# First stage of a bidirectional mLSTM mixer: which projections accumulate while the modulated input is being made, and which engine makes the first two modulation tiles

## The chip, the cores and the metric

The kernel runs on one core of one Trainium2 chip. The metric is the device time of one execution in microseconds, taken as the median of several executions. The core's engines run their own instruction streams and meet through semaphores: TensorE (PE, with its weight loads as PEld), VectorE (DVE), ScalarE (ACT), GpSimd (POOL) and SyncE (SP), which issues the DMAs.

## The reference, cut to what matters

```python
mod = silu(c) @ w_mod + b_mod                  # 1024 -> 6*1024: sh1, sc1, ga1, sh2, sc2, ga2
mod_c = silu(c_ctx) @ w_mod + b_mod            # only csh1, csc1 are used
hx = rmsnorm(x, g_mix) * (1 + sc1) + sh1       # 1024 latent tokens x 1024
hc = rmsnorm(ctx, g_mix) * (1 + csc1) + csh1   # 256 context tokens
q, k, v, o, gates = split(h @ w_in)            # 4 heads: q, k of 128, v of 256; o of 1024; 16 gates
...                                            # mLSTM scans in both directions from the context state,
...                                            # readout, w_out, residual, ConvGLU with w_up and w_down
return rmsnorm(x, g_final)
```

Everything is float32. The change touches only what stands up to the gates' first scan (the rows on mod, hx, hc and the first part of `h @ w_in`).

## The kernel before, in words

A float32 product runs as three fast products (`mm3`): each factor is split into a high part (a cast by ACT) and a low part (a subtraction by DVE); `split` does that for a weight piece, `hx_make` for the modulated input. The hidden dimension of 1024 is cut into eight k tiles of 128. `hxh[k]` and `hxl[k]` hold k tile k for 256 context tokens followed by 1024 latent tokens.

The first stage makes these tiles. For each of eight token tiles, x is loaded, its sum of squares is taken on ACT (`normed`, L162), the scale is computed on POOL, x is scaled on ACT (L164), transposed on TensorE (`x_trans`, L175, eight 128x128 blocks into two PSUM tiles of the tag s0, which has two buffers), and copied by ACT into `xT` (L176). Beside it the two modulation vectors are made group by group (`GROUPS`: k tile 0, k tile 1, then pairs). `mod_load` fetches eight row blocks of w_mod for the group's columns into `mr` pieces (3 buffers); `mod_acc` has DVE add them, each times its element of silu(c) (L207 the first, L209 the others); `mod_done` has TensorE sum over the partitions with a vector of ones (L218) and DVE add the bias and gains (L221, L222). Only then can `hx_make` modulate k tile k on DVE (L229), cast on ACT (L230) and subtract on DVE (L231).

While the tiles arrive, `start_mm` accumulates v and o of head 0 (512 columns) for the first NT0 = 6 token tiles in six PSUM tiles `ac`, k tile by k tile; the weights are split per pair of k tiles (`vo_split`). After the last k tile come, from line 816 on (`cmods`, `gates_w` and the loop behind them): v and o of the last two token tiles (`pv`), q of head 0 (`pq`), the gates (`pg`, with a 32-column weight and 512 tokens moving), k of head 0 (`pk`), and between them the sums for the context's two modulation vectors (`mod_sum`, 16 pieces of 128x1024, DVE L772, closed by `mod_cols`, L780). Then the context is normed and transposed (`ctx_x`, L501), its gates are made, `gate_cols` turns the gates to token-major by transposes (`gp`, L473), and `gate_rows` computes the scan's coefficients (`grp` L523 to `cp` L562) while k and v of the context and q of head 1 fill TensorE. The first product behind that is head 1's k on the context.

Instructions stand in each engine's queue in an order that a scheduler derives from the written order and from buffers; an engine takes them strictly in turn. `raw_tile` has 3 buffers, `wtile` 8.

Of the kernel before, what the change touches and what calls it, by code (L numbers as in the profile page):

```python
# [16 lines left out]
P = 128  # L17
# [22 lines left out]
def backbone(ctx, tc, x, c, ctxt, c_ctx, w_mod, b_mod, g_mix, g_ffn, w_in, b_gate,  # L40
# [92 lines left out]
    vp = tc.alloc_tile_pool(name="vp", bufs=1, side="right")  # L133
# [22 lines left out]
    def x_load(t):
        xt[t] = sp.tile([P, D], F32, tag="x", bufs=3, name=f"xt{t}")
        nc.sync.dma_start(out=xt[t], in_=x[t * P:(t + 1) * P, :])

    def normed(a, junk, ms, name):  # L160
# [21 lines left out]
    def mod_load(g, i):  # L182

        ks = GROUPS[g]
        n = len(ks) * P
        nk = 512 // n
        m_ = sp.tile([P, nk, 2, n], F32, tag="mr", bufs=3, name=f"mr{g}_{i}")
# [4 lines left out]
        pieces[g, i] = m_  # L192

# [17 lines left out]
    def mod_done(g):  # L211

        ks = GROUPS[g]
        p_ = s0(f"mc{g}")
        for w in range(2):
            for i, k in enumerate(ks):
                j = w * len(ks) + i
                T.matmul(p_[:, 2 * j:2 * j + 2], accs[g][:, j * P:(j + 1) * P], ones[:, 0:2], start=True, stop=True)  # L218
        for i, k in enumerate(ks):
            j = len(ks) + i  # L220
            V.tensor_tensor(out=hmod[:, k, 0:1], in0=p_[:, 2 * i:2 * i + 1], in1=bmc[:, k:k + 1], op=ALU.add)  # L221
            V.scalar_tensor_tensor(out=smod[:, k, 0:1], in0=p_[:, 2 * j:2 * j + 1], scalar=b1[:, k:k + 1],  # L222
                                   in1=gmix[:, k:k + 1], op0=ALU.add, op1=ALU.mult)

    def hx_make(k, a, b):

        v_ = xT[:, k, a * P:b * P]
        h_, l_ = [q[k][:, CTX + a * P:CTX + b * P] for q in (hxh, hxl)]
        V.tensor_scalar(out=v_, in0=v_, scalar1=smod[:, k, 0:1], scalar2=hmod[:, k, 0:1], op0=ALU.mult, op1=ALU.add)  # L229
        S.copy(h_, v_)  # L230
        V.tensor_tensor(out=l_, in0=v_, in1=h_.bitcast(F32), op=ALU.subtract)  # L231

# [12 lines left out]

    NT0 = 6
    ac = [ps0.tile([P, 512], F32, tag="ac", bufs=NT0, name=f"ac{t}") for t in range(NT0)]
    w0 = []
# [78 lines left out]
    x_load(6)
    mod_acc(3, 2)
    mod_load(4, 0)
    w0 += vo_split(0, 2, raws[2])  # L330
    x_load(7)
    mod_acc(3, 3)
    mod_load(4, 1)
    mod_done(3)
    for k in (4, 5):
        hx_make(k, 0, NT0)
        start_mm(k, range(NT0))
        x_norm(k + 2)
# [50 lines left out]
    for t in range(NT0):  # L389
        vo_out(0, t + 2, ac[t])  # L390
# [33 lines left out]
    def proj_t(h, key, sls, wts=None):  # L424

        off, scale = (OFF_Q, 1.0) if key == "q" else (OFF_K, DK ** -0.5)
        dst = hd[h].get(key)
        if dst is None:
            dst = hp.tile([P, SEQ if key == "q" else TOK], F32, tag=f"{key}T", bufs=2, name=f"{key}T{h}")
            hd[h][key] = dst  # L430
        c0 = CTX if key == "q" else 0
        wh, wl = wts or wcols(off + h * DK, DK, f"w{key}{h}_")
        hd[h][key, "w"] = wh, wl
        for o, n in sls:
# [5 lines left out]
            S.mul(dst[:, o - c0:o - c0 + n], p_[:, :n], scale)  # L440
# [5 lines left out]


    gts = hp.tile([P, TOK], F32, tag="kT", bufs=2, name="gts")[:32, :]
    wg = hp.tile([P, KT, 32], F32R, tag="mb", bufs=4, name="wg")

    def gates_w():
        r_ = hp.tile([P, KT, 16], F32, tag="mb", bufs=4, name="wgr")
        nc.sync.dma_start(out=r_, in_=kp(w_in[:, OFF_G:OFF_G + 16]))
        S.copy(wg[:, :, 0:16], r_)
        V.tensor_tensor(out=wg[:, :, 16:32], in0=r_, in1=wg[:, :, 0:16].bitcast(F32), op=ALU.subtract)
        nc.sync.dma_start(out=bgate, in_=b_gate[0].partition_broadcast(P))

    def gates(sls):
        for o, n in sls:
            p_ = pj(f"pg{o}")  # L460
            for k in range(KT):
                T.matmul(p_[:32, :n], wg[:, k, :], hxh[k][:, o:o + n], start=k == 0, stop=False)
                T.matmul(p_[:32, :n], wg[:, k, :], hxl[k][:, o:o + n], start=False, stop=k == KT - 1)
                if k == 3:
                    yield
            S.copy(gts[:, o:o + n], p_[:32, :n])
            yield

    def gate_cols():

        gp = st("gp")
        for t in range(NCH):
# [878 lines left out]
```

## Time and profile before

| | |
|---|---|
| median of 3 executions | 1258.0 us (1257.34 to 1263.27) |
| the profiled execution's own time | 1259.66 us |
| its span, first to last instruction | 1257.9 us |
| TensorE busy | 1196.4 us, 95% |
| VectorE busy | 917.6 us, 73% |
| ScalarE busy | 521.5 us, 41% |

The profile is of one execution. Its page gives the engines' busy time and, in 40 slices of the span, the busy share and TensorE's granted clock. From the trace behind it come a table by stretches, the waits of each engine with what ended them, groups of instructions with their mean duration, and a timeline of single instructions. A matmul's duration reaches into the next one; its cost in a stream is the distance of two starts.

### The profile page before, as it was taken

How to read it: one execution, taken by the hardware profiler on the slowest of the kernel's cores; microseconds unless marked ns; L12 is line 12 of the kernel's file. 1: busy time of each engine (PE TensorE's matmuls, PEld its weight loads, DVE VectorE, ACT ScalarE, POOL GpSimd, SP SyncE). 2: the span in 40 equal slices, each digit the busy share in tenths (PEclk: the TensorE clock that was granted, in tenths of full speed). 3: DMA queues.
4: the chain of work that ended last, by engine and by line, in shares of the span. 5: the costliest groups of instructions: out<-in, count | busy, mean ns of one | idle time of the engine just before them, and what ended most of it. 6: DMA issues, size and time to landing. Idle time of an engine off the chain costs nothing. (4 is left out here: it accounts for less than half of the span.)

```text
span 1257.9 us, 15855 instructions
## 1 busy us (share of the span) xinstructions
PE 1196.4 (95%) x5657; PEld 986.9 (78%) x5657; DVE 917.6 (73%) x1575; ACT 521.5 (41%) x931; POOL 83.6 (7%) x212
## 2 busy tenths in 40 slices
PE   4998899999999998989899999999999999999996
PEld 3775788888888877878668888888888888888885
DVE  5774587488557437846898777777978877895787
ACT  6531646344335434426643333332333324444452
POOL 1100001001101100101500000000000000000001
PEclk9898899999999999999899999999999999999998
DMA  8735551066323107123123322325354469624523
GB/s 250 258 100 188 173 178 49 27 191 201 112 67 109 51 9 258 52 84 128 57 84 101 101 72 80 101 67 198 127 177 167 134 217 388 249 95 144 184 71 117
DMA packets 132067, 170.35 MB, mean 135 GB/s; under 512 B 8718, under 2 KB 93966, under 8 KB 131988
## 3 DMA queue, kind: packets, MB, share of 16 engines
q1 hardware_dynamic: 131988, 169.34, 40.9%
q8 instruction: 44, 0.72, 0.2%
q14 instruction: 35, 0.29, 0.1%
HBM read 134.67 MB, written 34.64 MB: 135 GB/s over the span
## 5 line engine op out<-in xcount | busy, mean ns | idle before, releaser
L1082 ACT ACTIVATE t<-gt,cols 128x1024 f32<-128x1024 f32 x22 | 27.4, 1245 | 63.8 <-DVE gt L980 63.8
L980 DVE TENSOR_TENSOR e<-e,p 128x512 f32<-128x512 f32 x66 | 44.8, 680 | 9.5 <-PE p L87 9.3
L980 DVE TENSOR_TENSOR gt<-e,p 128x512 f32<-128x512 f32 x66 | 44.8, 680 | 6.5 <-PE p L87 6.4
L125 POOL TENSOR_SCALAR fms<-fms 128x1 f32<-128x1 f32 x8 | 3.8, 474 | 612.4 <-PE pa L87 589.0
L1088 ACT ACTIVATE t<-t 128x1024 f32<-128x1024 f32 x22 | 23.4, 1063 | 48.4 <-DVE t L1085 48.4
L85 PE MATMUL pk<-hxh,wk_0h 128*128 128x512 f32 (+1 forms) x96 | 35.8, 375 | 6.0 <-ACT wk_0h L80 6.0
L728 DVE SCALAR_TENSOR_TENSOR ha<-ha,hms,so 128x256 f32<-128x256 f32 x32 | 15.5, 485 | 32.9 <-POOL hms L126 32.2
L1083 DVE SCALAR_TENSOR_TENSOR t<-gt,cols,t 128x960 f32<-128x960 f32 x22 | 26.7, 1214 | 13.2 <-ACT t L1082 13.2
L86 PE MATMUL pk<-hxh,wk_0l 128*128 128x512 f32 (+1 forms) x96 | 35.3, 368 | 0.0
L87 PE MATMUL pk<-hxl,wk_0h 128*128 128x512 f32 (+1 forms) x96 | 34.8, 363 | 0.0
L85 PE MATMUL p<-bt,av 128*128 128x512 f32 x88 | 34.2, 389 | 0.0
L86 PE MATMUL p<-bt,av 128*128 128x512 f32 x88 | 34.2, 389 | 0.0
L87 PE MATMUL p<-bt,av 128*128 128x512 f32 x88 | 34.2, 389 | 0.0
L379 DVE TENSOR_TENSOR vl<-pv,vh 128x256 fp32r<-128x256 f32 x34 | 14.2, 417 | 26.2 <-ACT vh L378 26.2
L378 ACT CAST vh<-pv 128x256 fp32r<-128x256 f32 x34 | 12.6, 370 | 47.1 <-PE pv L87 46.8
L85 PE MATMUL nm<-vh,wh 128*128 128x258 f32 x64 | 29.9, 468 | 0.0
L636 DVE SCALAR_TENSOR_TENSOR kl<-kt,cco,kh 128x128 fp32r<-128x128 f32 x44 | 15.1, 346 | 18.6 <-ACT kh L635 18.5
L694 ACT ACTIVATE wi<-mb,bco 128x128 f32<-128x128 f32 x64 | 23.6, 397 | 12.1 <-PE nm L711 11.9
L721 ACT ACTIVATE ha<-nm,dn 128x256 f32<-128x256 f32 x32 | 15.1, 473 | 32.0 <-DVE dn L719 31.9
L980 DVE TENSOR_TENSOR sa<-rv 128x512 f32<-128x512 f32 x22 | 15.1, 687 | 18.2 <-DMA rv<-in_f_w_up_dram 18.2
L635 ACT ACTIVATE kh<-kt,cco 128x128 fp32r<-128x128 f32 x44 | 16.0, 370 | 27.9 <-PE kt L631 22.4
L1085 DVE SCALAR_TENSOR_TENSOR t<-gt,cols,t 128x960 f32<-128x960 f32 x22 | 26.6, 1210 | 0.0
(1065 smaller groups left out, 4187.0 us busy)
## 6 DMA issues: line engine op xcount, KB each, us to landing
rg<-in_f_w_up_dram SPq DMA_DIRECT2D x24, 512.0 KB, 3.7
rv<-in_f_w_up_dram SPq DMA_DIRECT2D x22, 512.0 KB, 4.2
actd<-t SPq DMA_DIRECT2D x22, 512.0 KB, 3.2
dr<-in_f_w_down_dram SPq DMA_DIRECT2D x44, 256.0 KB, 5.2
dr<-sums SPq DMA_DIRECT2D x44, 256.0 KB, 3.7
dr<-actd SPq DMA_DIRECT2D x33, 256.0 KB, 5.1
mr<-in_w_mod_dram SPq DMA_DIRECT2D x32, 256.0 KB, 4.1
vor<-in_a_w_in_dram SPq DMA_DIRECT2D x32, 256.0 KB, 3.3
```

What stands on the lines that cost most here:

```text
L85: T.matmul(ps, ah, bh, start=first, stop=False)
L86: T.matmul(ps, al, bh, start=False, stop=False)
L87: T.matmul(ps, ah, bl, start=False, stop=last)
L635: S.mul(kh, tp[:, c0:c0 + P], wc)
L636: V.scalar_tensor_tensor(out=kl, in0=tp[:, c0:c0 + P], scalar=wc, in1=kh.bitcast(F32), op0=ALU.mult, op1=ALU.subtract)
L694: S.activation(out=wi[:, d, :], in_=mrow_, func=AF.Exp, scale=-1.0, bias=mpco[:, cc:cc + 1])
L728: V.scalar_tensor_tensor(out=ha, in0=ha, scalar=ms[:, 1:2], in1=so[i], op0=ALU.mult, op1=ALU.mult)
L980: V.tensor_tensor(out=out_, in0=a_, in1=b_, op=op)
L1082: S.activation(out=t_, in_=gate, func=AF.Identity, scale=wcv[:, NFF + ff:NFF + ff + 1], bias=bcv[:, ff:ff + 1])
L1083: V.scalar_tensor_tensor(out=t_[:, GRID_W:], in0=gate[:, :SEQ - GRID_W], scalar=wcv[:, ff:ff + 1], in1=t_[:, GRID_W:], op0=ALU.mult, op1=A ...
L1085: V.scalar_tensor_tensor(out=t_[:, :SEQ - GRID_W], in0=gate[:, GRID_W:], scalar=wcv[:, 2 * NFF + ff:2 * NFF + ff + 1], in1=t_[:, :SEQ - GR ...
L1088: S.activation(out=t_, in_=t_, func=AF.Silu)
```

## The change

`start_mm` accumulates other projections along with the k tiles: q of head 0 and k of head 0 for both halves of the latent tokens, and q of head 1 for the first half (five `ac` tiles), with weights of 768 columns per pair of k tiles (`qk_load`, `qk_split`). The gates of the latent tokens go along too, token-major (`gate_mm`): the token tile is the weight, the 32 gate columns move, two products per k tile and token tile, into the PSUM tile `gb`. v and o of head 0 come behind the stage for all eight token tiles, after the second half of q of head 1 (`pq1b`).

The modulation vectors of k tiles 0 and 1 are made by TensorE for c and c_ctx together (`mod_pe`, `mod_pe_fin`); their w_mod pieces go first on the queue, for group 0 into `ga1` and `ga2`, which later serve as accumulators. The context's vectors are then summed for 768 columns only. Groups 2 to 4 keep DVE's sums, but each group is issued one earlier than before, so that its sum stands ready. `mr` has 5 buffers, `xt` 4. The scaling of x moves from ACT to DVE, as do half of the copies into `xT`. `hx_make` works on halves of 512 tokens.

```diff
     def x_norm(t):
-        normed(xt[t], ...)                       # ended in S.mul(a, a, ms[:, 1:2])
+        sumsq(xt[t], ..., ms)
+        V.tensor_scalar(out=xt[t], in0=xt[t], scalar1=ms[:, 1:2], scalar2=None, op0=ALU.mult)
...
-            S.copy(xT[:, k4 * 4:k4 * 4 + 4, t * P:(t + 1) * P], tp.rearrange("p (k n) -> p k n", k=4))
+            if k4 == 0:
+                S.copy(dst, tp4)
+            else:
+                V.tensor_copy(dst, tp4)
...
+    def mod_pe(g):
+        k, p_ = GROUPS[g][0], s0(f"mk{g}")
+        for w in range(2):
+            for j in range(KT):
+                T.matmul(p_[:, 2 * w:2 * w + 2], pieces[g, j // 4][:, j % 4, w, :], sct[:, j, :],
+                         start=j == 0, stop=j == KT - 1)
+        return p_
...
-    def hx_make(k, a, b):
+    def hx_make(k, s):
+        h_, l_ = [q[k][:, CTX + s * 512:CTX + (s + 1) * 512] for q in (hxh, hxl)]
...
-    NT0 = 6
-    ac = [ps0.tile([P, 512], F32, tag="ac", bufs=NT0, name=f"ac{t}") for t in range(NT0)]
-    def start_mm(k, ts):
-        for t in ts:
-            sl = slice(CTX + t * P, CTX + (t + 1) * P)
-            mm3(ac[t], hxh[k][:, sl], hxl[k][:, sl], *w0[k], k == 0, k == KT - 1)
+    ACC = {(0, 0): 0, (1, 0): 1, (2, 0): 2, (0, 1): 3, (1, 1): 4}
+    def qk_mm(p_, k, i, s):
+        sl = slice(CTX + s * 512, CTX + (s + 1) * 512)
+        mm3(p_, *w0[k][i], hxh[k][:, sl], hxl[k][:, sl], k == 0, k == KT - 1)
+    def gate_mm(p_, k, tt, start, stop):
+        sl = slice(tt * P, (tt + 1) * P)
+        T.matmul(p_, hxh[k][:, sl], wg[:, k, :], start=start, stop=False)
+        T.matmul(p_, hxl[k][:, sl], wg[:, k, :], start=False, stop=stop)
...
-    for _ in chain(proj_vo(0, (8, 9), w0), proj_t(0, "q", LSL), gates(LSL), proj_t(0, "k", LSL)):
-        next(cmods, None)
-    run(cmods)
-    run(ctx_x())
-    run(gates([(0, CTX)]))
+    cmods = chain(mod_sum(1, "mc1", mod_cols(smod[:, :, 1], gmix), ga1, 1, 256),
+                  mod_sum(0, "mc0", mod_cols(hmod[:, :, 1]), ga2, 1, 256))
+    vo_raw = [vo_load(0, 0)]
+    take(cmods, 2)
+    p_ = pj("pq1b")
+    for k in range(KT):
+        qk_mm(p_, k, 2, 1)
...
+    vo0 = proj_vo(0, list(range(2, NCH)) + [1, 0], wvo)
+    for _ in range(8):
+        take(vo0, 1)
+        take(cmods, 2)
+    run(cmods)
+    cx = ctx_x()
+    for _ in cx:
+        take(vo0, 1)
+    gates_ctx()
     gate_cols()
-    weave(gate_rows(), chain(proj_t(0, "k", [(0, CTX)], hd[0]["k", "w"]), proj_v_ctx(0), proj_t(1, "q", LSL)))
+    weave(gate_rows(), chain(vo0, proj_t(0, "k", [(0, CTX)])))
```

On TensorE the program's start stood so before (pr and pc turn the small vectors, tp is a transposition of x, mc a sum over partitions, ac an accumulation of v and o):

```order
L261 MATMUL pr<-ident,crow 128x16
L265 MATMUL pc<-ident,rows 128x128
L266 MATMUL pc<-ident,brow 128x48
L175 MATMUL tp_0_188<-ident,xt_140 128x128 x4
L175 MATMUL tp_1_194<-ident,xt_140 128x128 x4
L218 MATMUL mc_200<-ones,acc_168 128x2 x2
L175 MATMUL tp_0_209<-ident,xt_145 128x128 x4
L175 MATMUL tp_1_215<-ident,xt_145 128x128 x4
L85 MATMUL ac_134<-vo_0h,hxh_96 128x512
```

Now it stands so, with mk the modulation products of k tiles 0 and 1:

```order
L321 MATMUL pr<-ident,crow 128x16
L205 MATMUL mk_185<-vec,ga_91 128x2 x4
L205 MATMUL mk_185<-vec,ga_92 128x2 x4
...
L173 MATMUL tp_0_214<-ident,xt_137 128x128 x4
L173 MATMUL tp_1_220<-ident,xt_137 128x128 x4
L329 MATMUL pc<-ident,rows 128x128
L330 MATMUL pc<-ident,brow 128x48
L173 MATMUL tp_0_234<-ident,xt_139 128x128 x4
L173 MATMUL tp_1_240<-ident,xt_139 128x128 x4
L205 MATMUL mk_250<-vec,mr_0_147 128x2 x4
```

The modulation products of both groups stand ahead of the first accumulation, and so do the transposes of five token tiles instead of two.

On DVE the start read before:

```order
L768 MEMSET ga_91 128x1024
L267 COPY cols<-pc 128x128
L268 COPY bmc<-pc 128x48
L270 TENSOR_SCALAR bmc<-bmc 128x8
L207 TENSOR_SCALAR acc_168<-mr_0_142,vec 128x256
L209 SCALAR_TENSOR_TENSOR acc_168<-mr_0_142,vec,acc_168 128x256 x3
L209 SCALAR_TENSOR_TENSOR acc_168<-mr_1_147,vec,acc_168 128x256 x4
L221 TENSOR_TENSOR vec<-mc_200,bmc 128x1
```

and reads now (ms is the scale of a token tile, vec holds silu(c) and the modulation vectors):

```order
L166 TENSOR_SCALAR xt_137<-xt_137,ms_202 128x1024
L844 MEMSET ga_91 128x768
L166 TENSOR_SCALAR xt_139<-xt_139,ms_208 128x1024
L844 MEMSET ga_92 128x768
L179 COPY xT<-tp_1_220 128x4x128
L331 COPY cols<-pc 128x128
L332 COPY bmc<-pc 128x48
L334 TENSOR_SCALAR bmc<-bmc 128x8
L211 TENSOR_SCALAR vec<-mk_185,bmc 128x2
L212 TENSOR_SCALAR vec<-mk_185,bmc,cols 128x2
L179 COPY xT<-tp_1_240 128x4x128
L211 TENSOR_SCALAR vec<-mk_250,bmc 128x2
```

The eight accumulations of group 0 are gone from the place; the scalings and copies of x came in, and the memset of ga_91, which overwrites what the mk products read, stands ahead of the second scaling.

Where the fourth group (acc_520 before, acc_518 after, k tiles 4 and 5) is closed, DVE had before:

```order
L209 SCALAR_TENSOR_TENSOR acc_520<-mr_3_558,vec,acc_520 128x512
L229 TENSOR_SCALAR xT<-xT,vec 128x256
L221 TENSOR_TENSOR vec<-mc_593,bmc 128x1
L222 SCALAR_TENSOR_TENSOR vec<-mc_593,bmc,cols 128x1
L221 TENSOR_TENSOR vec<-mc_593,bmc 128x1
```

and has now:

```order
L230 SCALAR_TENSOR_TENSOR acc_518<-mr_3_483,vec,acc_518 128x512
L230 SCALAR_TENSOR_TENSOR acc_642<-mr_1_585,vec,acc_642 128x512
L230 SCALAR_TENSOR_TENSOR acc_518<-mr_3_483,vec,acc_518 128x512
L230 SCALAR_TENSOR_TENSOR acc_642<-mr_1_585,vec,acc_642 128x512
L241 TENSOR_TENSOR vec<-mc_563,bmc 128x2
L242 TENSOR_TENSOR vec<-mc_563,bmc 128x2
L230 SCALAR_TENSOR_TENSOR acc_642<-mr_2_588,vec,acc_642 128x512
```

Accumulations of the last group (acc_642) now stand between the fourth group's last ones and ahead of the reading of its sum (mc_563).

## Rows read from the trace of the kernel before

**Rows 1.** The page: busy time of the engines, TensorE's granted clock in 40 slices, and the chain that ended last.
```profile
PE 1196.4 (95%) x5657; PEld 986.9 (78%) x5657; DVE 917.6 (73%) x1575; ACT 521.5 (41%) x931; POOL 83.6 (7%) x212
...
PEclk9898899999999999999899999999999999999998
```

**Rows 2.** Four stretches from the program's start: the stretch, its length, the busy time of PE, PEld, DVE, ACT and POOL (instructions in brackets), granted clock of TensorE, DMA share, GB/s.
```profile
0.00:20.08 20.08, 5.73 (x24) 4.53 (x24) 9.37 (x25) 10.65 (x16) 3.28 (x32) 1.00 0.83 250
20.08:78.75 58.67, 51.74 (x221) 41.15 (x222) 43.95 (x91) 33.86 (x58) 6.38 (x12) 0.88 0.60 196
78.75:164.61 85.86, 74.11 (x377) 59.17 (x376) 50.34 (x83) 31.74 (x57) 1.49 (x4) 0.92 0.55 173
164.61:300.00 135.39, 134.14 (x758) 114.68 (x757) 96.98 (x254) 65.08 (x183) 13.38 (x54) 1.00 0.39 117
```

**Rows 3.** Timeline of PE: start, duration, what, idle time before it and what ended it. The first accumulation, the last product of the stage with the first two behind it, and the product behind which both programs are the same.
```profile
20.08 1.22 PE L85 MATMUL ac<-vo_0h,hxh 128*128 128x512 f32 x2 [0.98 <-ACT hxh L230]
...
78.52 0.39 PE L87 MATMUL ac<-vo_3l,hxh 128*128 128x512 f32 x1
78.75 0.39 PE L85 MATMUL pv<-vo_0h,hxh 128*128 128x512 f32 x1
78.97 0.39 PE L86 MATMUL pv<-vo_0h,hxl 128*128 128x512 f32 x1
...
164.61 0.28 PE L85 MATMUL pk<-hxh,wk_0h 128*128 128x256 f32 x1
```

**Rows 4.** Waits of DVE from 0 to 78.75 us, and of PE from 78.75 to 164.7: who waited for whom, total us, times, longest.
```profile
DVE vec L221 <- PE mc L218: 8.8, 5, 3.3
DVE acc L207 <- DMA mr<-in_w_mod_dram: 3.9, 1, 3.9
...
PE pk L85 <- ACT wk_0h L80: 6.0, 1, 6.0
PE tc L501 <- ACT xc L164: 3.6, 2, 3.5
PE cp L562 <- DVE gs L556: 1.1, 1, 1.1
PE pq L86 <- DVE wq_0l L81: 0.8, 1, 0.8
```

**Rows 5.** Timeline of ACT at the start: the first sum of squares, its read-out, the table load and silu.
```profile
7.30 1.06 ACT L162 ACTIVATE sq<-xt 128x1024 bf16<-128x1024 f32 x1 [5.30 <-DMA xt<-in_x_dram]
8.26 0.19 ACT L162 ACTIVATION_READ_ACCUMULATOR sq<-xt 128x1 f32 x1
8.46 1.28 ACT L263 ACT_TABLE_LOAD   x1
9.76 0.18 ACT L263 ACTIVATE vec<-pr 128x16 f32<-128x16 f32 x1
```

**Rows 6.** Timeline of PE: runs of transposes and of two-column products, early and late in the stage, and one run behind it.
```profile
11.03 1.97 PE L175 MATMUL tp<-ident,xt 128*128 128x128 f32 x8 [5.20 <-ACT xt L164]
16.30 0.98 PE L218 MATMUL mc<-ones,acc 128*128 128x2 f32 x4 [3.31 <-DVE acc L209]
40.77 0.95 PE L218 MATMUL mc<-ones,acc 128*128 128x2 f32 x8
103.94 1.84 PE L780 MATMUL mcp<-ones,mc 128*128 128x2 f32 x16
```

**Rows 7.** Groups of DVE and ACT instructions, each shape apart: line, engine, operation, tiles, shape, count, busy us, mean ns, idle before.
```profile
L209 DVE SCALAR_TENSOR_TENSOR acc<-mr,vec,acc 128x256 f32<-128x256 f32 x14 | 6.8, 484 | 2.3 <-DMA mr<-in_w_mod_dram 1.8
L207 DVE TENSOR_SCALAR acc<-mr,vec 128x256 f32<-128x256 f32 x2 | 0.7, 350 | 3.9 <-DMA mr<-in_w_mod_dram 3.9
L164 ACT ACTIVATE xt<-xt,ms 128x1024 f32<-128x1024 f32 x8 | 9.2, 1148 | 5.9 <-POOL ms L126 5.9
L176 ACT COPY xT<-tp 128x512 f32<-128x512 f32 x16 | 9.0, 582 | 3.8 <-PE tp L175 3.8
L267 DVE COPY cols<-pc 128x128 f32<-128x128 f32 x1 | 0.3, 292 | 2.3 <-PE pc L266 2.3
L648 DVE COPY cb<-dc 128x258 f32<-128x258 f32 x4 | 1.7, 427 | 0.6 <-PE dc L87 0.4
L945 DVE TENSOR_SCALAR xn<-x,ms 128x1024 f32<-128x1024 f32 x8 | 6.0, 754 | 4.6 <-POOL ms L126 4.4
L231 DVE TENSOR_TENSOR hxl<-xT,hxh 128x512 fp32r<-128x512 f32 x1 | 0.7, 683 | 0.0
```

**Rows 8.** Timeline of DVE where it has no gap: the distance of two starts is what an instruction costs in a full queue.
```profile
42.74 0.48 DVE L207 TENSOR_SCALAR acc<-mr,vec 128x512 f32<-128x512 f32 x1
43.14 0.67 DVE L229 TENSOR_SCALAR xT<-xT,vec 128x768 f32<-128x768 f32 x1
43.73 0.95 DVE L231 TENSOR_TENSOR hxl<-xT,hxh 128x768 fp32r<-128x768 f32 x1
44.60 0.75 DVE L209 SCALAR_TENSOR_TENSOR acc<-mr,vec,acc 128x512 f32<-128x512 f32 x1
...
47.27 4.68 DVE L209 SCALAR_TENSOR_TENSOR acc<-mr,vec,acc 128x512 f32<-128x512 f32 x6
```

**Rows 9.** Timeline of PE behind the stage: 32x32 transposes, two 256-column products in a stream, and the ends of the gate chain.
```profile
145.20 0.80 PE L473 MATMUL gp<-ident,gts 32*128 32x32 f32 x10
147.46 0.28 PE L85 MATMUL pv<-wv_1h,hxh 128*128 128x256 f32 x1
147.58 0.28 PE L86 MATMUL pv<-wv_1h,hxl 128*128 128x256 f32 x1
150.22 0.60 PE L523 MATMUL grp<-ident,gt 128*40 128x128 f32 x4
164.12 0.23 PE L562 MATMUL cp<-ident,gs 40*2 40x40 f32 x2 [1.06 <-DVE gs L556]
```

**Rows 10.** Timeline of PE late in the stage: six products behind a wait.
```profile
68.82 2.35 PE L85 MATMUL ac<-vo_3h,hxh 128*128 128x512 f32 x6 [2.02 <-ACT hxh L230]
```

**Rows 11.** All instructions of line 772 on the tile mc from 75 to 135 us: durations (least, median, most), first and last start.
```profile
L772 DVE SCALAR_TENSOR_TENSOR mc<-mc1r,vec,mc x8: 1278/1284/1287, 81.1 to 97.1; 128x1024 f32<-128x1024 f32 x8
```

More of the change, by code (lines that the diff above doesn't have):

```diff
@@ new lines, in backbone @@
+    mod_load(1, 0)
+    mod_load(1, 1)
+    raws = [qk_load(0)]
+    nc.sync.dma_start(out=wgr, in_=kp(w_in[:, OFF_G:OFF_G + 16]))
+    x_load(2)
+    x_load(3)
+    x_load(4)
+    for i in range(4):
+        mod_load(2, i)
+    raws.append(qk_load(1))
+    x_load(5)
+    pr = s0("pr")
+    T.transpose(pr[:, :2 * KT], crow, ident[:2 * KT, :2 * KT])
+    S.activation(out=sct, in_=pr[:, :2 * KT].rearrange("p (w k) -> p k w", w=2), func=AF.Silu)
+    mk = mod_pe(0)
+    x_norm(0)
+    x_norm(1)
+    x_trans(0)
@@ new lines, in backbone @@
+    pc = s0("pc")
+    T.transpose(pc[:, 0:P], rows, ident)
+    T.transpose(pc[:, P:P + 48], brow, ident[:48, :48])
+    V.tensor_copy(cols, pc[:, 0:P])
+    V.tensor_copy(bmc, pc[:, P:P + 48])
+    b1 = bmc[:, 8:16]
+    V.tensor_scalar(out=b1, in0=b1, scalar1=1.0, scalar2=None, op0=ALU.add)
+    mod_pe_fin(0, mk)
+    x_trans(1)
+    x_load(6)
+    x_load(7)
+    mk = mod_pe(1)
+    mod_pe_fin(1, mk)
+    qk_split(0, raws[0])
+    make_wg(wg, wgr)
+    x_norm(2)
+    x_trans(2)
+    x_norm(3)
@@ new lines, in backbone @@
+    x_trans(3)
+    hx_make(0, 0)
+    start_mm(0, 0)
+    x_norm(4)
+    hx_make(1, 0)
+    start_mm(1, 0)
+    x_trans(4)
+    mod_acc(2, 0)
+    mod_acc(2, 1)
+    gates_mm(0, 0)
+    gates_mm(1, 0)
+    x_norm(5)
+    x_trans(5)
+    mod_acc(2, 2)
+    mod_acc(2, 3)
+    qk_split(1, raws[1])
+    mc = mod_sums(2)
+    x_norm(6)
+    mod_fin(2, mc)
+    hx_make(2, 0)
+    x_trans(6)
+    start_mm(2, 0)
+    x_norm(7)
+    hx_make(3, 0)
+    x_trans(7)
+    start_mm(3, 0)
+    hx_make(0, 1)
+    hx_make(1, 1)
@@ new lines, in backbone @@
+    for i in range(4):
+        mod_load(3, i)
+    raws.append(qk_load(2))
+    for k in (0, 1):
+        start_mm(k, 1)
+        gates_mm(k, 1)
+    mod_acc(3, 0)
+    hx_make(2, 1)
+    mod_acc(3, 1)
+    hx_make(3, 1)
+    gates_mm(2, 0)
+    gates_mm(3, 0)
+    start_mm(2, 1)
+    gates_mm(2, 1)
+    mod_acc(3, 2)
+    mod_acc(3, 3)
+    mc = mod_sums(3)
+    start_mm(3, 1)
+    gates_mm(3, 1)
+    for g in (3, 4):
+        a, b = GROUPS[g]
+        if g == 3:
+            for i in range(4):
+                mod_load(4, i)
+            raws.append(qk_load(3))
+        mod_fin(g, mc)
+        qk_split(g - 1, raws[g - 1])
+        hx_make(a, 0)
+        hx_make(a, 1)
+        for s in range(2):
+            start_mm(a, s)
+            gates_mm(a, s)
+        if g == 3:
+            mod_acc(4, 0)
+            mod_acc(4, 1)
+        hx_make(b, 0)
+        hx_make(b, 1)
+        start_mm(b, 0)
+        gates_mm(b, 0)
+        if g == 3:
+            mod_acc(4, 2)
+            mod_acc(4, 3)
+            mc = mod_sums(4)
+        start_mm(b, 1)
+        gates_mm(b, 1)
@@ L424, in proj_t @@
     def proj_t(h, key, sls, wts=None):
[L426 to L433, printed above, removed]
+        if key not in hd[h]:
+            qk_tile(h, key)
+        wh, wl = wts or wcols((OFF_Q if key == "q" else OFF_K) + h * DK, DK, f"w{key}{h}_")
         for o, n in sls:
@@ L458, in gates @@
[L458 to L480 removed]
+    nc.sync.dma_start(out=bgate, in_=b_gate[0].partition_broadcast(P))
```

283 lines of the change are left out of this document (123 added, 160 removed).

## Prediction

> **What bounds the kernel now.** I read the page first: TensorE is busy 95% of the span, with the granted clock below 90% in slices 2, 4, 5, 20 and 40 of the 40 [rows 1]. So time can be won where TensorE idles, and that is at the start. The table by stretches shows where [rows 2]. Behind 164.61 us TensorE is busy 134.14 of 135.39 us. In the 164.61 us before it is busy 5.73 + 51.74 + 74.11 = 131.6. The product at 164.61, head 1's k on the context, is the anchor: the programs are the same behind it, and there TensorE is full, so I carry a shift of the anchor to the end unchanged. The question is where the anchor lands.
>
> Three stretches matter. Up to 20.08 nothing accumulates [rows 3]. From there to 78.75 the last k tile is being made, and DVE, which makes the k tiles, is busy 43.95 of 58.67 us (75%); its largest wait is for the sums that TensorE makes over the partitions, 8.8 us in five waits, the longest 3.3 [rows 2, 4]. From 78.75 TensorE loses 11.7 us to waits, 6.0 of it for the cast of k's weights and 3.6 for the context's tokens [rows 4]. The change goes at all three.
>
> **The start.** Silu(c) is ready at 9.94 us: x0 lands at 7.30, then 1.06 + 0.19 for the sum of squares, 1.28 for the table load, 0.18 [rows 5]. The changed order puts 1 MB of w_mod ahead of x0. At the 250 GB/s of this stretch [rows 2] that is 4 us; issues of small vectors that stood ahead move behind, so x0 lands near 9 and silu(c) is ready near 11.9 (11 to 13). Group 0's modulation is 16 fp32 products, two records each (a pair of mc products made four records): 32 records at 0.245 us early in the stage (0.98 / 4) or 0.119 later (0.95 / 8) [rows 6], so 7.8 or 3.8 us, and 5.8 between. Then the two PSUM buffers of tag s0 make a ladder. The 16 transposes of x0 and x1 cost 16 x 0.246 = 3.9 (1.97 / 8) [rows 6], with ACT's copy of 0.58 [rows 7] and DVE's copy and small readers between, some 1.5. DVE's memset of ga1 also waits until the products have read it, with x1's scaling queued behind, on which the transposes of x1 and group 1's products hang; I take 1.5 for that, between nothing and 3. Group 1's products are another 3.8 to 7.8, say 5. That puts k tile 1's vectors at 11.9 + 5.8 + 6 + 1.5 + 5 = about 30; I take 31 with the semaphore steps, 28 to 34. DVE must then still split the first weights, scale x2 to x4 and make the first hx, some 7 us of its queue, so the first accumulation comes near 38, against 20.08.
>
> **The rest of the stage.** What counts is when DVE has group 4's vectors, for the last two k tiles wait for them. In a gapless stretch DVE's cost is the distance of starts: 0.40 for a 512-column scalar operation (42.74 to 43.14), 0.87 for a 768-column subtraction (43.73 to 44.60), 4.68 / 6 = 0.78 for a chained accumulation [rows 8]. Behind 31 us its queue holds:
> - 24 accumulations of groups 2 to 4: 21 x 0.78 + 3 x 0.40 = 17.6
> - 6 scalings of x, 1024 wide: the nearest row is 0.754 [rows 7], 0.67 by distance, so 4.0. On ACT they cost 1.15 each
> - 6 copies out of PSUM, 512 wide: between 0.427 for 258 columns and its extrapolation from 128 columns (0.292), 0.69 [rows 7], 0.61 by distance: 3.7
> - 4 weight splits of 768 columns: 4 x 0.87 = 3.5
> - hx for k tiles 0 to 5, both halves: 12 x 0.42 + 12 x 0.60 (0.683 less the overlap) [rows 7, 8] = 12.2
> - closings, the gate weights and two early pieces for the context: 3.2
>
> Together 44.2 us. The scalings and copies, all eight token tiles, are 11 us of new DVE work; what leaves is groups 0 and 1, 14 x 0.484 + 2 x 0.350 = 7.5 us [rows 7]. So DVE does not get lighter. What the change can win is its waits for TensorE: without the part of the 8.8 us that lies behind 20.08 (7.6), DVE's share before would have been 43.95 / 51 = 86%. With the sums a group ahead I take 88%: 44.2 / 0.88 = 50.2, so group 4's vectors come at 81. Behind them stand the last two k tiles on TensorE: 30 products at 0.227 (distance of starts at 78.52, 78.75, 78.97 [rows 3]) and 32 gate products, plus 1.2 for the first hx.
>
> **Gate products.** No row has a 128-column weight with 32 columns moving. The nearest are the two-column fp32 products at 0.115 to 0.119 a record [rows 6] and 256 columns at 0.118 [rows 9]; on the other side the 32x32 transposes at 0.08 [rows 9], and less can't be excluded. I take 0.115, nearest in weight width. There are 160: 128 in the stage (14.7 us, three quarters of it beside waiting) and 32 for the context. Before, the gates cost about 32 x 0.23 + 16 x 0.118 + 0.8 = 10. By these rows the token-major form costs TensorE 8 us more in products, of which only the last k tiles' 3.7 and the context's 3.7 lie on the path.
>
> The Trainium skill has a rule that speaks against this form (TensorE: Matmul & The Clock Gate, section LDWEIGHTS): a weight load goes by its columns, P / 1.2 ns, some 107 ns for 128, however few columns then move. The rows' 0.115 for two columns agree. By the same page's issue gap for up to 64 columns, some 25 ns, the 160 products would cost 4 us in place of 18, an estimate by that page.
>
> The stage so ends at 81.2 + 6.8 + 3.7 + 1.2 = 92.9 us. Before it ended at 78.75.
>
> **From there to the anchor.** TensorE's work: q of head 1, second half, 24 x 0.227 = 5.5; v and o of head 0, 192 x 0.227 = 43.6; two closings for the context, 24 records x 0.115 = 2.8; context transposes 1.8; its gates 3.7; v and k on the context, (48 + 24) x 0.118 = 8.5; the scan's small products 0.9. That is 66.8, where before it was 74.11 busy and 85.86 long [rows 2]. Stalls: the 6.0 us for k's weights go, because v and o's weights are cast during q's 5.5 us; the gate chain from grp to cp (13.9 us, 150.22 to 164.12 [rows 9]) has 11 to 12 us of fill and may leave 1. What is late next is the context's modulation. Its pieces share three raw buffers with four weight pieces that can be split only as q's weights fall free. Before, eight pieces took 16.0 us, start to start 2.3 [rows 11]; at three quarters of the width 1.7, so 14 pieces from about 7 us behind the stage's end are done at 31, against TensorE's arrival at 29. I take 2 for that, 1.5 for the context's tokens (3.6 before [rows 4]), 1 for the gate chain and 1.2 for a slower clock after waits: 72.5 (69 to 76).
>
> **Sum.** Anchor 92.9 + 72.5 = 165.4 against 164.61: +0.8 us. On the profiled execution, 1259.66, that is 1260.5; on the median, 1258.0, it is 1258.8. I forecast no change, 1259. Its own range takes the start (28 to 34), DVE's share (83 to 93%) and the tail together: -6 to +6, 1252 to 1265.
>
> **Rivals.**
> A. *DVE runs without gaps and the start is warm.* For it: three groups' accumulations lie in the queue as filling, and the gapless stretches show it can [rows 8]. Against it: hx goes DVE, ACT, DVE, and every closing still waits for TensorE; 7 us of idle time that were not waits for sums were left in the stage before. Price: vectors at 28.5 + 44.2 = 72.7, stage end 84.4, tail 70: anchor 154.4, 10 us early; with gate products at 0.08 another 2 to 3: about 1247.
> B. *TensorE runs at half speed through the stage's end.* It waits for each hx half, and after such a wait of 2.02 us before, six products took 2.35 us, 0.39 apart instead of 0.227 [rows 10]; the granted clock of the stretch was 0.88 [rows 2], between the levels of 1.2 and 2.4 GHz. If the last two k tiles run at 1.2 GHz they cost 21 instead of 10.5, so the anchor comes 11 us late: 1269. It decides from the point where over half of the last 12 us of the stage has the lower clock. Against it: k tiles 4 and 5 with their gates give TensorE 10 us of unbroken work just ahead.
> C. *The context's vectors hold TensorE up.* If its pieces come at the old pace of 2.3 us [rows 11], 14 take 32 us and TensorE waits 10 in place of 2: 1267.
> D. *The sums are not ahead.* In DVE's order the last group's final four accumulations stand behind the fourth group's reading, so one wait for TensorE remains; it costs at most the 3.3 of before [rows 4] and lies within the forecast.
>
> **How the numbers follow.** No change 0.42, A 0.28, B 0.17, C 0.13. A measurement of this kernel can tell 0.5%, 6.3 us. Faster by more is A, 0.28; slower by more is B and C, 0.30; the same 0.42. The range must leave out no more than two in ten, so it reaches to A's and B's times with their far edges cut off: 1247 to 1270.
>
> **What would show it.** In the changed kernel's trace: group 0's modulation at 12 to 19 us and the first accumulation at 36 to 41 (if before 30, the start was mispriced); DVE at 85 to 92% from 31 us to group 4's reading at 78 to 84; 0.11 to 0.12 us a gate product in a full stream; the stage's last product at 88 to 97; the first closing of the context's sums with a wait under 3 us; the anchor at 159 to 171. The forecast is wrong if DVE's work behind k tile 1 is not near 44 us, or if it does not set when the last k tiles start; then the stage's end moves by the whole difference.

## The result

The changed kernel takes 1268.8 us, median of 7 executions (1266.7 to 1272.8), against 1258.0 before: 1.0082 times as long, 95% interval 1.0061 to 1.0104. The profiled execution took 1267.05 us with a span of 1265.1, 7.2 more than before. The forecast of no change (1259) missed by more than its own bounds (1252 to 1265); the whole range, 1247 to 1270, holds the time, on the side of the slower rivals.

### The profile page after: what moved, and what is told of

It is laid out like the page before. It is cut to its first block, busy times and chain, and to the rows that moved or that the text cites. A ratio compares the mean times of both kernels' runs of the same rounds, so it can differ in the third digit from the quotient of the medians.

```text
span 1265.1 us, 16150 instructions
## 1 busy us (share of the span) xinstructions
PE 1206.9 (95%) x5807; PEld 1004.8 (79%) x5807; DVE 914.0 (72%) x1567; ACT 506.7 (40%) x910; POOL 77.4 (6%) x212
## 4 chain that ended last, share of the span: by engine, by line
PE 48%; DVE 3%; ACT 0%; POOL 0%; issue 0%; DVEq 0%; POOLq 0%; ACTq 0%
PE p L86 11%; PE p L87 11%; PE p L85 11%; PE pa L85 3%; PE pa L86 3%; PE pa L87 3%; PE pb L85 2%; PE pb L86 2%; PE pb L87 2%; DVE bt L1063 1%; DVE bs L1080 0%; DVE dr L1371 0%; DVE bu L1063 0%; DVE sb L1080 0%; DVE at0l L81 0%
## 5 line engine op out<-in xcount | busy, mean ns | idle before, releaser
L1188 ACT ACTIVATE t<-t 128x1024 f32<-128x1024 f32 x22 | 23.4, 1062 | 49.1 <-DVE t L1185 49.1
L1183 DVE SCALAR_TENSOR_TENSOR t<-gt,cols,t 128x960 f32<-128x960 f32 x22 | 26.7, 1215 | 13.3 <-ACT t L1182 13.3
L85 PE MATMUL pv<-vo_3h,hxh 128*128 128x512 f32 (+1 forms) x80 | 29.9, 374 | 1.3 <-ACT vo_3h L80 1.3
L87 PE MATMUL pv<-vo_3l,hxh 128*128 128x512 f32 (+1 forms) x80 | 29.8, 373 | 1.4 <-DVE vo_3l L81 1.4
L85 PE MATMUL pv<-vo_2h,hxh 128*128 128x512 f32 (+1 forms) x80 | 30.7, 384 | 0.0
L85 PE MATMUL pv<-vo_0h,hxh 128*128 128x512 f32 (+1 forms) x80 | 30.3, 378 | 0.0
L86 PE MATMUL pv<-vo_1h,hxl 128*128 128x512 f32 (+1 forms) x80 | 30.1, 377 | 0.0
L87 PE MATMUL pv<-vo_1l,hxh 128*128 128x512 f32 (+1 forms) x80 | 30.1, 376 | 0.0
L85 PE MATMUL pv<-vo_1h,hxh 128*128 128x512 f32 (+1 forms) x80 | 29.9, 374 | 0.0
L86 PE MATMUL pv<-vo_2h,hxl 128*128 128x512 f32 (+1 forms) x80 | 29.8, 373 | 0.0
L87 PE MATMUL pv<-vo_2l,hxh 128*128 128x512 f32 (+1 forms) x80 | 29.7, 371 | 0.0
```

Source lines behind the costliest of these rows:

```text
L85: T.matmul(ps, ah, bh, start=first, stop=False)
L86: T.matmul(ps, al, bh, start=False, stop=False)
L87: T.matmul(ps, ah, bl, start=False, stop=last)
L1183: V.scalar_tensor_tensor(out=t_[:, GRID_W:], in0=gate[:, :SEQ - GRID_W], scalar=wcv[:, ff:ff + 1], in1=t_[:, GRID_W:], op0=ALU.mult, op1=A ...
L1188: S.activation(out=t_, in_=t_, func=AF.Silu)
```

## The profile after

The page: busy time, and TensorE's granted clock in 40 slices.

```profile
PE 1206.9 (95%) x5807; PEld 1004.8 (79%) x5807; DVE 914.0 (72%) x1567; ACT 506.7 (40%) x910; POOL 77.4 (6%) x212
...
PEclk9899999999999999999999999999999999999999
```

Against [rows 1], TensorE is busy 10.5 us longer (1206.9 - 1196.4). The span grew by 7.2, so 3.3 us of idling are all that the change removed. That balance is the result in one line.

The table by stretches (columns as in [rows 2]): up to k tile 1's vectors, from there to the reading of group 4's sum, the last two k tiles, and the way to the anchor.

```profile
0.00:34.50 34.50, 18.84 (x83) 17.27 (x83) 5.98 (x19) 10.38 (x17) 4.92 (x18) 1.00 0.67 205
34.50:89.49 54.99, 46.72 (x245) 39.98 (x246) 42.34 (x75) 15.81 (x27) 4.46 (x11) 0.88 0.59 176
88.40:102.08 13.68, 13.68 (x87) 12.14 (x86) 4.80 (x11) 4.18 (x8) 0.51 (x15) 1.00 0.06 6
102.08:173.48 71.40, 69.10 (x368) 58.49 (x368) 44.32 (x89) 30.65 (x56) 2.26 (x4) 0.98 0.47 144
```

DVE is busy 42.34 us where 44.2 was forecast, but in 55.0 us instead of 50.2: 77%, not 88%. TensorE is full from 88.40 to the stage's end, at the full clock. The timeline of PE shows the places: the two modulation runs, the first accumulation, the fourth group's sum and k tile 4, group 4's sum, the end of the stage, the closing of the context's first sum, and the anchor.

```profile
13.57 6.99 PE L205 MATMUL mk<-vec,ga 128*128 128x2 f32 x32 [10.68 <-ACT vec L323]
27.13 6.98 PE L205 MATMUL mk<-vec,mr 128*128 128x2 f32 x32
42.72 0.50 PE L85 MATMUL ac<-hxh,qk_h 128*128 128x512 f32 x1 [0.25 <-ACT hxh L250]
47.09 0.26 PE L286 MATMUL gb<-wg,hxh 128*128 128x32 f32 x1
47.20 0.26 PE L287 MATMUL gb<-wg,hxl 128*128 128x32 f32 x1
74.55 1.03 PE L235 MATMUL mc<-ones,acc 128*128 128x2 f32 x8
78.61 0.66 PE L85 MATMUL ac<-hxh,qk_h 128*128 128x512 f32 x1 [3.03 <-ACT hxh L250]
88.42 1.03 PE L235 MATMUL mc<-ones,acc 128*128 128x2 f32 x8
102.08 0.48 PE L85 MATMUL pq1b<-hxh,qk_h 128*128 128x512 f32 x1
121.16 1.50 PE L858 MATMUL mcp<-ones,ga 128*128 128x2 f32 x12 [1.60 <-DVE ga L849]
173.48 0.28 PE L85 MATMUL pk<-hxh,wk_0h 128*128 128x256 f32 x1
```

Against [rows 3], the first accumulation comes 22.6 us later, the stage ends 23.3 later, the anchor 8.9. The first run waits for silu, which ACT takes behind x0's sum of squares, and x0 lands at 10.88 us, against 7.30 in [rows 5]:

```profile
10.88 1.06 ACT L160 ACTIVATE sq<-xt 128x1024 bf16<-128x1024 f32 x1 [8.88 <-DMA xt<-in_x_dram]
12.04 1.28 ACT L323 ACT_TABLE_LOAD   x1
13.34 0.18 ACT L323 ACTIVATE vec<-pr 128x16 f32<-128x16 f32 x1
```

DVE's timeline around the last two sums:

```profile
66.73 4.06 DVE L230 SCALAR_TENSOR_TENSOR acc<-mr,vec,acc 128x512 f32<-128x512 f32 x6
75.62 0.16 DVE L241 TENSOR_TENSOR vec<-mc,bmc 128x2 f32<-128x2 f32 x1 [4.83 <-PE mc L235]
...
84.79 0.74 DVE L230 SCALAR_TENSOR_TENSOR acc<-mr,vec,acc 128x512 f32<-128x512 f32 x1
89.49 0.16 DVE L241 TENSOR_TENSOR vec<-mc,bmc 128x2 f32<-128x2 f32 x1 [3.96 <-PE mc L235]
```

Its waits for such sums up to 102 us, as in [rows 4]:

```profile
DVE vec L241 <- PE mc L235: 10.1, 3, 4.8
```

DVE had done the accumulations of these two groups by 70.8 and at 85.5 us. The sums stood ready in its order, but on TensorE they came at 74.55 and 88.42, behind accumulations and gate products of earlier k tiles. The wait that [rows 4] show as 8.8 us is 10.1 now.

## The experiments

The columns: first accumulation, end of the stage (start of `pq1b`), anchor and span of the one profiled execution in us, and the ratio to the kernel before over all executions with its interval.

| run | first acc. | stage end | anchor | span | ratio |
|---|---|---|---|---|---|
| before | 20.1 | 78.8 | 164.6 | 1257.9 | 1 |
| changed | 42.7 | 102.1 | 173.5 | 1265.1 | 1.0082 [1.0061, 1.0104] |
| mk_half | 35.4 | 92.4 | 163.6 | 1258.5 | 1.0036 [1.0021, 1.0051] |
| silu_first | 36.3 | 95.7 | 169.9 | 1262.2 | 1.0036 [1.0016, 1.0055] |
| gates_late | 41.9 | 107.3 | 177.1 | 1271.3 | 1.0131 [1.0116, 1.0147] |
| mod_dve | 33.4 | 92.7 | 165.3 | 1261.5 | 1.0061 [1.0037, 1.0084] |
| gates_half | 41.7 | 97.2 | 168.4 | 1261.1 | 1.0051 [1.0034, 1.0067] |
| gates_hold | 41.7 | 106.3 | 177.5 | 1270.9 | 1.0113 [1.0082, 1.0145] |
| dve_silu | 30.3 | 97.9 | 172.1 | 1265.7 | 1.0037 [1.0019, 1.0054] |
| dve_silu_hold | 31.1 | 92.7 | 166.3 | 1262.6 | 1.0046 [1.0029, 1.0062] |
| old_gates | 42.0 | 91.7 | 170.5 | 1266.2 | 1.0065 [1.0046, 1.0083] |
| dve_old | 34.0 | 83.0 | 165.6 | 1258.1 | 1.0013 [1.0001, 1.0025] |
| dve_x_old | 33.0 | 84.9 | 164.4 | 1256.1 | 1.0031 [1.0017, 1.0046] |
| dve_silu_old | 29.7 | 80.5 | 161.8 | 1254.3 | 0.9991 [0.9974, 1.0007] |

A profile shows one execution, and those of one kernel here spread by up to 12 us (dve_silu: 1255.5 to 1267.5, the profiled one the longest). So stages are compared by the profiles, and versions by the ratios. The two do not rank the versions alike: silu_first has a later anchor than mod_dve, but a lower ratio.

**mk_half.** Half of each modulation run.

```diff
-            for j in range(KT):
+            for j in range(KT // 2):
```

> Each of the two TensorE modulation runs sums over only the first half of the hidden dimension (8 of 16 products, the rest of the sum is left out), so each run takes 3.5 us instead of 7.0. Theory 1 (the late start): from the first accumulation at 42.7 us on, TensorE is idle only 5.4 of 59 us, so whatever delays that accumulation delays the anchor; it should come near 36 and the anchor (head 1's k on the context, 173.5 in the changed kernel) near 167, the time 6 to 7 us lower. Rival (loads and DVE set the pace of the stage, the start has slack): the anchor moves by less than 2 us.

The first accumulation came 7.3 us earlier, the anchor 9.9, the span is 6.6 shorter, and the ratio's interval lies apart from the changed kernel's. The start has no slack.

**silu_first.** A tiny DVE write, which needs silu(c), goes into the tile that the first sum of squares writes, so ACT's order turns.

```diff
+    V.tensor_scalar(out=first[:, 0:1], in0=sct[:, 0, 0:1], scalar1=1.0, scalar2=None, op0=ALU.mult)
+    sumsq(xt[0], first, ms0)
-    x_norm(0)
```

> Silu of c stands ahead of the first sum of squares on ACT, so it no longer waits for x0 and one table load falls away. Theory 1: the first modulation run starts when its w_mod pieces land, near 9 us instead of 13.6, the first accumulation comes 4 to 5 us earlier and the anchor with it. Rival (the start has slack): under 1 us.

The timeline of PE in this run:

```profile
4.55 1.84 PE L205 MATMUL mk<-vec,ga 128*128 128x2 f32 x8 [1.67 <-DMA ga<-in_w_mod_dram]
7.09 5.28 PE L205 MATMUL mk<-vec,ga 128*128 128x2 f32 x24 [0.70 <-DMA ga<-in_w_mod_dram]
```

The run starts at 4.55, where the pieces land, not near 9. First accumulation and stage end came 6.4 us earlier, the anchor 3.6: the stage gives it on in full, the way behind it gives 2.8 back (74.2 us instead of 71.4, at a granted clock of 0.93). The ratio's interval lies apart from the changed kernel's, as mk_half's does: this order on ACT alone, with no part of the change undone, gives back about half of the loss. DVE's waits for the sums and the stretch from k tile 1's vectors to group 4's reading stayed as they were:

```profile
DVE vec L241 <- PE mc L235: 10.1, 3, 4.9
28.05:83.07 55.02, 46.77 (x245) 39.99 (x246) 42.35 (x75) 15.82 (x27) 4.47 (x11) 0.88 0.57 176
```

**gates_late.** All calls of `gates_mm` are written behind the last k tile.

```diff
-            gates_mm(a, s)
...
+    for k in range(KT):
+        for s in range(2):
+            gates_mm(k, s)
```

> All 128 gate products of the latent tokens stand behind the last k tile, none among the accumulations. Theory 1 (TensorE is full from the first accumulation on): the same work in another place, the anchor within 2 us of 173.5, since what the sums win ahead of them is lost as 14 us of uncovered gates. Theory 2 (the sums of groups 3 and 4 stand on TensorE behind the gates, DVE waits 4.8 and 4.0 us for them, and this back and forth sets the stage's end): the waits fall below 2 us each and the anchor comes 4 to 5 us earlier.

Neither happened, and the edit did something else: the scheduler drew the products forward and bunched them ahead of the fourth group's sum. In the table by stretches:

```profile
57.00:77.70 20.70, 20.70 (x101) 18.45 (x99) 13.23 (x22) 4.07 (x7) 0.00 (x0) 0.75 0.39 120
```

And in PE's timeline, within the bunch:

```profile
71.72 0.26 PE L286 MATMUL gb<-wg,hxh 128*128 128x32 f32 x1
71.83 0.26 PE L287 MATMUL gb<-wg,hxl 128*128 128x32 f32 x1
71.94 0.36 PE L286 MATMUL gb<-wg,hxh 128*128 128x32 f32 x1
72.14 0.37 PE L287 MATMUL gb<-wg,hxl 128*128 128x32 f32 x1
72.35 0.37 PE L286 MATMUL gb<-wg,hxh 128*128 128x32 f32 x1
```

The sum came at 77.69 instead of 74.55, and the anchor 3.6 us later. Within the bunch the distance of products rose from 0.11 to 0.21 us: some 28 products in, the clock fell to half. So the sum's later place and the slower products come together here, and this run alone does not tell them apart; gates_half moves the sum the other way.

**mod_dve.** One part undone, for group 0 as for group 1 shown here.

```diff
-    mk = mod_pe(1)
-    mod_pe_fin(1, mk)
+    mod_acc(1, 0)
+    mod_acc(1, 1)
+    mod_fin(1, mod_sums(1))
...
-    mod_sum(1, "mc1", mod_cols(smod[:, :, 1], gmix), ga1, 1, 256)
+    mod_sum(1, "mc1", mod_cols(smod[:, :, 1], gmix), ga1, 1, 0)
```

> Undoes one part: k tiles 0 and 1 get their modulation from DVE's accumulations as in the kernel before (the loads keep the changed order), and the context's vectors are summed full width again. Theory 1: TensorE loses 14 us of products ahead of the first accumulation, which comes near 34 instead of 42.7, and the anchor comes 6 to 8 us earlier in spite of 7.5 us more on DVE. Rival (DVE is the bound of the stage): the anchor stays or comes up to 4 us later.

First accumulation 33.4 us, anchor 8.2 earlier, as theory 1 had it; DVE's 7.5 us more did not bind. The time follows only in part (span 3.6 shorter; the ratios' intervals overlap).

**gates_half.** The calls for k tiles 0 to 3 are left out but for the first.

```diff
-    gates_mm(1, 0)
...
-        gates_mm(k, 1)
...
-    gates_mm(2, 0)
-    gates_mm(3, 0)
...
-    gates_mm(2, 1)
...
-    gates_mm(3, 1)
```

> Leaves out 56 of the 128 latent gate products, all that stand ahead of the third group's successor sum (k tiles 0 to 3 but for one block), so the gates are incomplete; 56 x 0.112 = 6.2 us of TensorE work is gone. What the run with the gates moved showed has changed the second theory: the scheduler bunched the products ahead of the fourth group's sum, which came 4 us later after the same start, and the anchor went back 3.6 us. Theory 1 (TensorE's total of work from the first accumulation on sets the end): anchor 173.5 - 6.2 = 167.3. Theory 2 (the chain fourth group's sum, DVE, first hx of k tile 4 sets the end, and DVE has that group's accumulations done only near 70.5): the sum can move from 74.6 to about 71, the anchor by 3.5 to 4, to 169.7, and TensorE idles the rest away.

The fourth group's sum waits for DVE now:

```profile
69.12 1.05 PE L235 MATMUL mc<-ones,acc 128*128 128x2 f32 x8 [0.79 <-DVE acc L230]
```

The run's first accumulation is 1.1 us earlier, as starts differ from execution to execution; corrected by that, the sum came 4.4 us earlier and the anchor 4.0, not 6.2. That is theory 2 for this stretch: DVE's accumulations bound the sum, and the rest of the saved work becomes idle time.

**gates_hold.** 32 products use `wgb`, a copy of the weight that is made only after the fourth group's sum.

```diff
+            wgb = sp.tile([P, KT, 32], F32R, name="wgb")
+            V.tensor_scalar(out=wgb[:, 0, 0:1], in0=smod[:, 4, 0:1], scalar1=1.0, scalar2=None, op0=ALU.mult)
+            S.copy(wgb, wg.bitcast(F32))
+            for k, s in ((2, 0), (3, 0), (2, 1), (3, 1)):
+                gates_mm(k, s)
```

> 32 of the gate products, those of k tiles 2 and 3, are held back behind the fourth group's sum by giving them a copy of their weight that is written only after it; they fill the 3.0 us in which TensorE waits for k tile 4. The work is the same. Theory 2: the sum comes near 71, the wait of 3.0 us is filled, the anchor 3 to 4 us earlier (about 170). Theory 1 in its strict form (no idle time worth having): under 1 us.

The sum did come at 71.08, and then the gain was lost. PE's timeline behind it:

```profile
74.44 0.28 PE L290 MATMUL gb<-wgb,hxh 128*128 128x32 f32 x1 [2.42 <-ACT wgb L404]
...
75.58 0.26 PE L290 MATMUL gb<-wgb,hxh 128*128 128x32 f32 x1
...
76.09 0.37 PE L291 MATMUL gb<-wgb,hxl 128*128 128x32 f32 x1
```

The table by stretches, from this sum to the next, here and then in the changed kernel:

```profile
71.08:92.66 21.58, 19.16 (x90) 17.23 (x88) 9.96 (x19) 2.68 (x5) 0.48 (x7) 0.68 0.25 74
74.55:88.42 13.87, 10.84 (x58) 9.30 (x58) 9.91 (x18) 2.28 (x4) 0.29 (x5) 0.88 0.36 104
```

The copy of the weight came late, so a wait of 2.42 us stayed, and the products behind it were soon 0.213 apart. The granted clock was 0.68 over the stretch (0.88 in the changed kernel's), which took 21.6 us instead of 13.9.

**dve_silu** and **dve_silu_hold.** The edits of mod_dve and silu_first together, and these with that of gates_hold.

> Two parts together: k tiles 0 and 1 summed on DVE as before, and silu of c ahead of the first sum of squares on ACT, so that those sums begin when the first w_mod pieces land (near 7 us) instead of at 13. Theory 1: first accumulation near 27 to 29 us (33.4 with DVE's sums alone), anchor 160 to 161, time 0.3% below the kernel before. Rival: from there on the loads of x and w_mod set the pace and the anchor moves by under 2 us from 165.3.

> All three: DVE's sums for k tiles 0 and 1, silu first, and 32 gate products held back behind the fourth group's sum. If the parts add up, the anchor is at 157 to 158, some 7 us ahead of the kernel before, and the time 1251 (0.5% faster). If loads or DVE take over as the bound, it stays at the anchor of the version without the held gates.

The start moved by less than expected (30.3 and 31.1 us, for 27 to 29), and the end of the stage came no earlier (97.9 and 92.7, against 92.7). In dve_silu's profiled execution the stretch between the last two sums took 19.7 us where mod_dve's took 14.5, with the same products in the same order but for one gate product and three accumulations more. First dve_silu's stretch, then mod_dve's; the granted clock is 0.65 and 0.88:

```profile
61.81:81.49 19.68, 16.78 (x65) 14.27 (x65) 11.19 (x19) 2.28 (x4) 0.13 (x2) 0.65 0.27 80
64.99:79.50 14.51, 11.49 (x62) 9.88 (x62) 10.44 (x18) 2.28 (x4) 0.13 (x2) 0.88 0.36 108
```

Over all executions dve_silu's ratio is below mod_dve's (1.0037, 1.0061), but the intervals overlap, so a gain is not shown. The expectations of 0.997 and 0.995 failed.

**old_gates, dve_old, dve_x_old, dve_silu_old.** The gates behind the stage with the gate columns as weight, alone and with the earlier edits; in dve_x_old, to which the last hunk belongs, x0 and x1 are loaded between the w_mod pieces, x0 first.

```diff
-            gates_mm(a, s)
...
+            T.matmul(g_[:32, :n], wg[:, k, :], hxh[k][:, o:o + n], start=k == 0, stop=False)
+            T.matmul(g_[:32, :n], wg[:, k, :], hxl[k][:, o:o + n], start=False, stop=k == KT - 1)
...
-    mod_load(0, 0)
-    mod_load(0, 1)
-    x_load(0)
-    x_load(1)
+    x_load(0)
+    mod_load(0, 0)
+    x_load(1)
+    mod_load(0, 1)
```

> Undoes another part: the latent tokens' gates are made as before, behind the stage, with the 32 gate columns as weight and 512 tokens moving (32 products at 0.23 us and 8 small transposes, 8 us) in place of 128 token-major products at 0.112 us (14.3 us) in the stage. If TensorE's work sets the end, 14.3 - 8.0 = 6.3 us less: anchor near 167. If the token-major products only cover waits for the next k tile, the stage shortens by less than the 8 us that come behind it, and the anchor stays at 173 or comes later.

> Both undone: k tiles 0 and 1 summed on DVE, and the gates made as before. If the two add up: 8.2 us from the first (anchor 165.3 alone) and what the gates alone give, 4 to 6 us: anchor 159 to 161, time 0.2 to 0.4% below the kernel before. If DVE, with 7.5 us more, becomes the bound of the stage, nothing beyond 165.

> As the last, and the loads begin with x0, then half of the first w_mod pieces, x1, the other half, as before. x0 lands near 7 instead of 11 us, so its transposition starts 3 to 4 us earlier; the sums on DVE can begin at 10. If the start sets the rest: first accumulation near 30 instead of 33.4, anchor 2 to 3 us earlier than without it. If the granted clock falls in the waits that this opens, the gain is lost, as with silu put first on top of DVE's sums.

> DVE's sums for k tiles 0 and 1, silu ahead of the first sum of squares, and the gates as before. With the token-major gates the version with the first two had its fourth group's stretch run at a granted clock of 0.65 and lost its early start. If the narrow products are what keeps the clock down after a wait, this one keeps it up: first accumulation near 30, anchor 157 to 160, 0.3 to 0.5% faster than the kernel before. If the waits alone do it, the anchor is at 165 or later.

In old_gates DVE's waits for the sums fall from 10.1 to 4.5 us, and DVE needs 49.1 us from k tile 1's vectors to group 4's reading, 86% of them busy:

```profile
DVE vec L239 <- PE mc L233: 4.5, 3, 2.8
33.95:83.05 49.10, 37.91 (x162) 30.73 (x162) 42.03 (x74) 15.82 (x27) 4.71 (x11) 0.83 0.64 196
```

Its stage is 9.6 us shorter (first accumulation corrected by 0.8) for 14.3 us of products gone, so a third of them had covered waits. The old form is paid behind the stage (78.9 us from there to the anchor instead of 71.4), and the anchor gains 2.2. With both parts undone the ratio is 1.0013, apart from the changed kernel's interval and within 0.5% of the kernel before. dve_x_old started only 1.0 us earlier and gained nothing. dve_silu_old has the earliest anchor, 161.8, and 0.9991: not to be told from the kernel before. Its anchor lies between the two expectations. Without narrow products in the stage the granted clock between its last two sums was still only 0.74, behind the same wait of 3.0 us for k tile 4, so the narrow products alone are not what holds the clock down. No version here beats the kernel before by what can be measured.

## Why the prediction was right or wrong

**The balance.** The anchor came at 173.5, forecast 165.4: 8.1 us. By terms: k tile 1's vectors 34.5 for 31 (+3.5), from there to group 4's reading 55.0 for 50.2 (+4.8), the last two k tiles 12.6 for 11.7 (+0.9), the way to the anchor 71.4 for 72.5 (-1.1).

**The start** was mis-sized: silu at 13.5 for 11.9 and modulation runs of 7.0 us each, at 0.218 a record, for 5.8 and 5; the slow end of the bounds, 0.245 a record, was the nearer. That the first accumulation would come some 18 us later and that this would be on the path was right, and mk_half, silu_first and mod_dve show it. What was too kind is how much of it would be made good by shorter waits behind.

**The failed step** is DVE's share: "With the sums a group ahead I take 88%". It came to 77%, since DVE waited 4.8 and 4.0 us for the last two sums. The sums are ahead in DVE's order alone. TensorE takes its queue in turn: from 57.65 us on it idled only 3.0 us until the stage's end, and the sums stood behind other products. What puts them behind is above all the gate products, and not the late start. With the start 6.4 us earlier (silu_first) the two waits are 4.9 and 3.9 and the stretch is 55.0 us as before; without the gate products (old_gates) they are 0.5 and 2.8, the stretch is 49.1 and DVE's share 86%, near the forecast 50.2 and 88%. So the premise under **Gate products**, that three quarters of them run beside waiting, fails together with this share. Rival D came nearest: it expected one wait for the last group's sum, from DVE's order, of at most 3.3 us; there were two, and TensorE's order made them. gates_half moves the fourth group's sum 4.4 us earlier and the anchor follows by 4.0.

**Gate products**: taken at 0.115, measured 0.11 (47.09 to 47.20). The Trainium skill's rule on weight loads (TensorE: Matmul & The Clock Gate, section LDWEIGHTS), 107 ns for 128 columns, agrees with that at the full clock; at half of it the products stood 0.213 apart (gates_hold), which the rule does not give, so the agreement alone does not show that the weight load sets the pace. The issue gap of some 25 ns on the same page of the Trainium skill (section Back-to-back issue gap) is not what a product cost here. That a quarter of the stage's gates would be on the path was too low: two thirds were, by old_gates's one profile.

**The rivals.** B is refuted: the last 13.7 us of the stage ran at a granted clock of 1.00, and the halved clock stood ahead of them, 78.6 to 82.1. C is refuted: the first closing waited 1.6 us, and the tail was shorter than forecast. A was wrong in its start (34.5 for 28.5) and right of DVE only in part: from 34.5 to 70.8 DVE had just 3.7 us of gaps, but the two waits of 8.8 us came behind. B and C named the right size for wrong reasons, and as the range reached to B's time, it is luck that it holds the measured one.

**What settles the cause.** TensorE modulation of two k tiles and token-major gates, undone together, bring the time back to 1.0013. Each alone gives a quarter to a third of that (1.0061, 1.0065), with intervals that overlap the changed kernel's; so the two are shown together, and the share of each in the time is not settled (by the centres, the two gains add up to little more than half of the joint one). In the traces they act at different places: the modulation runs set the first accumulation (33.4 us without them), the gate products the waits for the sums. The rest of the change (q and k in place of v and o in the stage, x's scaling on DVE, sums a group ahead) nets to the 0.0013 that is left, with an interval of 0.0001 to 0.0025: next to nothing, and no gain. Why it gains nothing though it removes two waits of 6.0 and 3.6 us behind the stage (2.0 of the second are left in dve_old) was not tried apart; dve_old's first accumulation still comes 14 us later than that of the kernel before.

## What to carry to other kernels

A sum issued a group ahead is ahead only if the engine that makes it has it ahead of other work in its own queue; check both engines' orders. Moving work onto the engine that bounds the program pays only where it idles and nothing waits behind it: fourteen microseconds of small products at the start delayed everything that followed. And price a narrow product by one of the same weight width in the trace, not by its columns: with a 128-column weight, 2 and 32 moving columns both cost 0.11 us here at the full clock.

## What the runs showed of the hardware

The two-column fp32 products of the start stood 0.218 us apart, against 0.11 late in the stage (eight of them from 88.42 to 89.31), while the table's granted clock reads 1.00 for the first 34.5 us; there the distance of starts shows the rate, not that column.

A run of products with 32 moving columns lost the full clock while it was unbroken (gates_late), or soon after a wait (gates_hold), and it stayed lost for 13.6 us, over wide products too; behind the 3.0 us wait of the changed kernel, with 512 columns moving, it was back after 3.5. But dve_silu shows 12.5 us at half speed behind its wait, wide products and groups of eight narrow ones in turn, in an order in which mod_dve had the full clock back after 3.2. Ahead of that wait dve_silu had also run at half speed from about 55.0 to 61.5 us, behind 24 narrow products in a row that mod_dve passed at the full clock. What decides between the two is left open.
